# A fixed order for the expert pairs, with the gather one pair ahead and the overflow branch moved

## The chip, the cores and the metric

The kernel runs on one core of a Trainium2 chip (trn2). The metric is the device time of one execution in microseconds (us); less is better.

## The reference

One block of a network on 256 tokens of width 2048, all in float32. A vector `c` gives shifts, scales and gates through `silu(c) @ w_ada + b_ada`.

```
h  = rmsnorm(x) * (1 + sc1) + sh1;  proj = h @ w_in             # 2048 x 7192
mix = [gated delta rule (8 heads), forgetting attention (8 heads)] @ w_out
x  = x + g1 * mix
h2 = rmsnorm(x) * (1 + sc2) + sh2
# experts: top-1 of 4 groups, then top-2 of the 8 experts of that group
y  = sum over chosen e of weight_e * (silu(h2 @ w1[e]) * (h2 @ w3[e])) @ w2[e]
out = rmsnorm(x + g2 * y)
```

There are 32 experts, each with `w1` and `w3` of 2048 x 512 and `w2` of 512 x 2048: 12 MB an expert. Every expert's weights are read, whichever tokens chose it.

## The kernel before

**Start.** `mod_T(n)` makes four rows of the first shift and scale from weight tiles `mt` (1 MB each, `ada_load`, line 204): of each pair of tiles VectorE takes one (`ada_dve`, lines 215 and 217) and TensorE the other (line 229). Both need `sc_t`, which is silu(c): one ScalarE activation (line 172) and three small VectorE instructions. ScalarE issues loads ahead of that activation: the constants `KC`, four quarters `xq` of x, the further constants `K`, the parameters `SM`, three rows into `MOD`; later `wab` (line 480). After all of `mod_T(0)` come the 16 `x_transpose` (line 199) and `mod_fin(0)` (line 243), then the projection with weight tiles `wr` (line 361; ScalarE and VectorE split each into two parts, lines 371 and 377). In this part the order on TensorE and SyncE is the order in which the code is written (`manual_schedule`); elsewhere a list scheduler that works with estimated times lays out each engine's instructions at build time, and may take later ones ahead. A DMA can also wait for an earlier DMA whose completion semaphore it takes over.

**Experts.** 16 pairs of experts, each with 64 token slots per expert. One-hot matrices are built on VectorE: `oh` (line 1217), `ohr` (1223, with the norm's factor), `ohw` (1220, with the weights). The rest of a pair is, on TensorE:

- gather: four times 8 matmuls by `ohr` (line 1229) into the PSUM tag `g` (two buffers), added on VectorE into `heT` (line 1230). The first quarter comes ahead of the pair's up projection, the others between its quarters (`GA = 1`);
- up: 64 matmuls into `h1` and `h3` (line 1249), the two experts of the pair in the two column halves of the array, so that two matmuls run side by side;
- hidden: tanh on ScalarE (1255), two VectorE instructions (1256, 1257), four transposes `pht` (1260) and two `pwt` of `ohw` (1265), copied by ScalarE into `hidT` (1262) and `ow` (1267);
- down: 32 matmuls into `po` (1290; for the last pair 1309, column block by column block), scaled by the gate on VectorE (`scale_out`, 1279);
- scatter: 8 matmuls `py` (1273), added on VectorE into `X2` (1275).

The profile counts each float32 matmul as two records. SyncE loads the weights in tiles of 1 MB (lines 1244, 1286, 1306), 24 a pair, into a ring of 17 slots (`r2t` nine, `r3t` eight) and at the first turn three tiles that borrow other buffers (`r4t`).

Tokens beyond 64 of an expert are left to `overflow`, a branch on the greatest count (`tc.If`, line 1162) with a loop over all experts inside. It stands ahead of pair 8 (`OVP = 8`, pairs counted from 0), uses SyncE loads into `r2t`, and isn't entered with these inputs.

```
    for pr in range(NE // 2):
        e0 = 2 * pr
        if pr == OVP:
            overflow()
        ...
        for q in range(4):
            if q + GA < 4:
                gather(q + GA)
            for hx, wr in ((h1, w1_r), (h3, w3_r)):
                ...
```

Of the kernel before, what the change touches and what calls it, by code (L numbers as in the profile page):

```python
# [7 lines left out]
F32 = mybir.dt.float32  # L8
# [8 lines left out]
P = 128  # L17
# [52 lines left out]
OVP = 8  # L70
# [10 lines left out]
C_LATE, C_W = 320, 992 + 3 * 128  # L81
# [29 lines left out]
def block_kernel(ctx: ExitStack, tc: tile.TileContext, x, w_mod, w_gate, w_in, w_ab, w_out, w_router, w1, w3, w2,  # L111
# [45 lines left out]
    def kc(c0, n):  # L157
        return K[:, c0 - C_LATE:c0 - C_LATE + n]
# [7 lines left out]
    nc.scalar.dma_start(K, consts[:, C_LATE:])  # L166
    nc.scalar.dma_start(SM, small.partition_broadcast(P))
    nc.scalar.dma_start(MOD[0:P:32], rows[:, 0:3])
# [291 lines left out]
    for _ in mod_T(0):  # L460
        pass
    for j in range(NJ):
        x_transpose(j)
    mod_fin(0)
    n_rot = 0
    for b in range(3):
        b_now[0] = b
        m = mod_T(b + 1)
        for c in range(7):
            for _ in range(MP[c]):  # L470
                next(m)
            if c == 6:
                mod_fin(b + 1)
            if c == 0:
                step(acc_k, "T", hHb, hLb, 0, NJ - 1)
            else:
                spilled(early[c], c, b, rot[n_rot % 2])
                n_rot += 1
        if b == 1:
            nc.scalar.dma_start(wab[:, :, 0:24], w_ab)  # L480
# [662 lines left out]
    def ring2_tile():  # L1143
        n = ring_n[0]
        ring_n[0] += 1
        if RB + RC <= n < RB + RC + 3:
            tag, bufs = (("heT", 2), ("ob", 1), ("g2b", 1))[n - RB - RC]
            return ep.tile([P, 2048], F32, name="r4t", tag=tag, bufs=bufs)
        if n >= RB + RC:
            n -= 3  # L1150
        if n % (RB + RC) >= RB:
            return ring3.tile([P, 2048], F32, name="r3t", tag="r3t")
        return ring2.tile([P, 2048], F32, name="r2t", tag="r2t")
# [6 lines left out]
    def overflow():  # L1160
        most = nc.values_load(cnt[0:1, 0:1], min_val=0, max_val=T)
        with tc.If(most > CAP):  # L1162
            dr = ep.tile([P, 2, P], F32, name="dr", tag="ow", bufs=1)
            for t in range(2):
                nc.vector.tensor_scalar(dr[:, t], ident, r2[:, t:t + 1], None, op0=OP.mult)
            hv = [ep.tile([P, 8, T], F32, name="hv", tag="heT", bufs=2) for _ in range(2)]
            for j in range(0, NJ, 2):
                pt = ps_g.tile([P, 2, T], F32, name="pth", tag="g")
                for a in range(2):
                    for t in range(2):  # L1170
                        nc.tensor.matmul(pt[:, a, t * P:(t + 1) * P], h2p[:, t, j + a], dr[:, t], start=True, stop=True)
                nc.vector.tensor_tensor(hv[j // 8][:, j % 8:j % 8 + 2], pt,
                                        S2[:, j:j + 2, None].to_broadcast([P, 2, T]), op=OP.add)
            with tc.For_i(0, NE, 1) as e:
                hp = [[ps_o.tile([P, 512], F32, name="hx", tag="o") for t in range(2)] for m in range(2)]
                for m, wr in enumerate((w1_r, w3_r)):
                    for q in range(4):
                        tl = ring2.tile([P, 2048], F32, name="r2t", tag="r2t").rearrange("p (j f) -> p j f", j=4)
                        nc.sync.dma_start(tl, wr[bass.ds(e, 1), :, 4 * q:4 * q + 4].rearrange("o p j f -> p (o j) f"))
                        for jj in range(4):  # L1180
                            j = 4 * q + jj
                            for t in range(2):
                                nc.tensor.matmul(hp[m][t], hv[j // 8][:, j % 8, t * P:(t + 1) * P], tl[:, jj],
                                                 start=j == 0, stop=j == NJ - 1)
                hT = ep.tile([P, 4, T], F32, name="vhT", tag="ob", bufs=1)
                for t in range(2):
                    th = ep.tile([P, 512], F32, name="vth", tag="eth", bufs=1)
                    nc.scalar.activation(th, hp[0][t], AF.Tanh, scale=0.5)
                    nc.vector.scalar_tensor_tensor(th, th, 1.0, hp[0][t], op0=OP.add, op1=OP.mult)
                    nc.vector.scalar_tensor_tensor(th, th, 0.5, hp[1][t], op0=OP.mult, op1=OP.mult)  # L1190
                    nc.vector.tensor_scalar(th, th, cof[:, t, bass.ds(e, 1)], None, op0=OP.mult)
                    pt = ps_g.tile([P, 4, P], F32, name="vpt", tag="g")
                    for c in range(4):
                        nc.tensor.transpose(pt[:, c], th[:, c * P:(c + 1) * P], ident)
                    nc.scalar.activation(hT[:, :, t * P:(t + 1) * P], pt, AF.Copy)
                wt = []
                for c in range(4):
                    tl = ring2.tile([P, 2048], F32, name="r2t", tag="r2t").rearrange("p (o d) -> p o d", o=1)
                    nc.sync.dma_start(tl, w2_r[bass.ds(e, 1), :, c].rearrange("o p d -> p o d"))
                    wt.append(tl)  # L1200
                for n in range(4):
                    for t in range(2):
                        py = ps_g.tile([P, 512], F32, name="vpy", tag="g")
                        for c in range(4):
                            nc.tensor.matmul(py, hT[:, c, t * P:(t + 1) * P], wt[c][:, 0, n * 512:(n + 1) * 512],
                                             start=c == 0, stop=c == 3)
                        vy = ep.tile([P, 512], F32, name="vy", tag="eth", bufs=1)
                        nc.vector.tensor_tensor(vy, py, g2b[n], op=OP.mult)
                        xs = X2[:, t, n * 512:(n + 1) * 512]
                        nc.vector.tensor_tensor(xs, xs, vy, op=OP.add)  # L1210

    for pr in range(NE // 2):
        e0 = 2 * pr
        if pr == OVP:
            overflow()
# [3 lines left out]
        ohw = ep.tile([P, 2, 2, SLOTS], F32, name="ohw", tag="ohw", bufs=1)  # L1219
        nc.vector.tensor_tensor(ohw, oh, comb[:, :, e0:e0 + 2, None].to_broadcast([P, 2, 2, SLOTS]), op=OP.mult)  # L1220
        heT = ep.tile([P, NJ, P], F32, name="heT", tag="heT", bufs=2)
        ohr = ep.tile([P, 2, 2, SLOTS], F32, name="ohr", tag="ohr", bufs=2)
        nc.vector.tensor_tensor(ohr.rearrange("p t a s -> p t (a s)"), oh.rearrange("p t a s -> p t (a s)"),
                                r2[:, :, None].to_broadcast([P, 2, 2 * SLOTS]), op=OP.mult)
        def gather(j4):
            pg_ = ps_g.tile([P, 4, P], F32, name="pgt", tag="g")
            for jj in range(4):
                for t in range(2):
                    nc.tensor.matmul(pg_[:, jj], h2p[:, t, 4 * j4 + jj], ohr[:, t], start=t == 0, stop=t == 1)  # L1229
            nc.vector.tensor_tensor(heT[:, 4 * j4:4 * j4 + 4], pg_,  # L1230
                                    S2[:, 4 * j4:4 * j4 + 4, None].to_broadcast([P, 4, P]), op=OP.add)

        h1 = ps_h.tile([P, 512], F32, name="h1", tag="h")
        h3 = ps_h.tile([P, 512], F32, name="h3", tag="h")
        for j4 in range(GA):
            gather(j4)
        for q in range(4):
            if q + GA < 4:
                gather(q + GA)
# [11 lines left out]
        if pr == NE // 2 - 1:  # L1251
            fgt = ep.tile([P, 2048], F32, name="fgb", tag="heT", bufs=2)
            fgb = [bcast(fgt[:, n * 512:(n + 1) * 512], MOD[:, 1], n) for n in range(4)]
# [3 lines left out]
        nc.vector.scalar_tensor_tensor(th, th, 0.5, h3, op0=OP.mult, op1=OP.mult)  # L1257
        pt = ps_g.tile([P, 4, P], F32, name="pht", tag="g")
# [8 lines left out]
        nc.scalar.activation(ow, pw, AF.Copy)  # L1267
        po = [ps_o.tile([P, 512], F32, name="po", tag="o") for _ in range(4)]
# [12 lines left out]
        if pr < NE // 2 - 1:  # L1281
# [11 lines left out]
            if pr == 0:  # L1293
                g2t = ep.tile([P, 2048], F32, name="g2b", tag="g2b", bufs=1)
                g2b = [bcast(g2t[:, n * 512:(n + 1) * 512], MOD[:, 2], n) for n in range(4)]
            for n in range(4):
                scale_out(n)
            for t in range(2):
                for n in range(4):
                    scatter(t, n)  # L1300
        else:
            for n in range(4):
                wt = [ring2_tile().rearrange("p (c f) -> p c f", c=4) for _ in range(2)]
                for cs in (slice(0, 2), slice(2, 4)):
                    for i in range(2):
                        nc.sync.dma_start(wt[i][:, cs], w2_r[e0 + i, :, cs, n * 512:(n + 1) * 512])
                for c in range(4):
                    for i in range(2):
                        nc.tensor.matmul(po[n][64 * i:64 * i + 64], hT[:, c, 64 * i:64 * i + 64], wt[i][:, c],  # L1309
# [11 lines left out]
    for t in range(2):  # L1321
        for n in range(4):
# [7 lines left out]
            if n % 2:  # L1330
                nc.sync.dma_start(out[0, t * P:(t + 1) * P, (n - 1) * 512:(n + 1) * 512],
                                  X2[:, t, (n - 1) * 512:(n + 1) * 512])
    est.close()
# [51 lines left out]
```

## Time and profile before

| what | value |
|---|---|
| time, median of 3 runs | 1703.01 us (1700.43 to 1703.21) |
| the profiled execution: its own time | 1703.19 us |
| its span, first to last instruction | 1701.4 us |
| TensorE busy in the span | 1575.6 us (93%) |
| VectorE, ScalarE, GpSimd busy | 39%, 19%, 7% |
| DMA over the span | 588.50 MB, mean 346 GB/s |
| mean granted TensorE clock | 0.978 of full speed |

Busy shares are means over the span: TensorE waits in the first 50 us and in the last 40, and is all but always busy between. The span leaves 1.8 us of the execution's own time outside it.

### The profile page before, as it was taken

The page shows a single profiled execution, that of the slowest core. Times are in us where ns is not written, and L with a number is a line of the kernel's source. Part 1 is how long each engine was busy: PE and PEld are TensorE (multiplying, and loading weights), DVE is VectorE, ACT ScalarE, POOL GpSimd, SP SyncE. Part 2 cuts the span into 40 slices and gives each one's busy share as a digit, 9 for nine tenths or more (in the row PEclk, how much of TensorE's full clock was granted, in tenths as well). Part 3 has the DMA queues.
Part 4 walks back from the last instruction along what each step waited for, and adds up shares of the span by engine and source line. Part 5 has one row for each costly group of instructions (what it writes and reads, how often), then busy time and mean ns, then how long its engine had stood idle before and what let it go on. Part 6 is the DMA issues. An engine that isn't in the chain of part 4 may idle for free. (4 is left out here: it accounts for less than half of the span.)

```text
span 1701.4 us, 20695 instructions
## 1 busy us (share of the span) xinstructions
PE 1575.6 (93%) x8430; PEld 892.4 (52%) x8430; DVE 663.4 (39%) x1038; ACT 327.8 (19%) x652; POOL 116.5 (7%) x140
## 2 busy tenths in 40 slices
PE   3999988899899988799999999999899999999996
PEld 1788857787678766433433443443443443343342
DVE  4677797766655644220221221222022122122022
ACT  2543553353334543100000000000000000000002
POOL 1000041332101021000000000000000000000001
PEclk9999999899999999799999999999999999999999
DMA  9989787787786475799999999994999999999993
GB/s 348 367 331 352 266 315 287 266 316 274 290 314 244 148 294 207 311 385 387 407 406 421 405 407 421 405 406 163 385 420 421 420 421 420 421 421 420 421 408 115
DMA packets 102038, 588.50 MB, mean 346 GB/s; under 512 B 16932, under 2 KB 17316, under 8 KB 41268
## 3 DMA queue, kind: packets, MB, share of 16 engines
q1 hardware_dynamic: 93916, 581.05, 85.2%
q10 hardware_dynamic: 8024, 6.09, 1.2%
q8 instruction: 68, 1.11, 0.3%
q14 instruction: 30, 0.25, 0.0%
HBM read 584.73 MB, written 2.10 MB: 345 GB/s over the span
## 5 line engine op out<-in xcount | busy, mean ns | idle before, releaser
L1249 PE MATMUL h<-r2t,heT 128*64 128x512 f32 x1088 | 270.1, 595 | 1.9 <-DMA r2t<-in_w_dram 1.9
L1249 PE MATMUL h<-r3t,heT 128*64 128x512 f32 x960 | 240.0, 594 | 0.0
L377 DVE TENSOR_TENSOR wL<-wr,wH 128x1024 fp32r<-128x1024 f32 x144 | 176.9, 1231 | 96.7 <-ACT wH L371 81.3
L371 ACT ACTIVATE wH<-wr 128x1024 fp32r<-128x1024 f32 x144 | 151.6, 1056 | 144.3 <-PE acc L408 70.0
L1255 ACT ACTIVATE eth<-h 128x512 f32<-128x512 f32 x16 | 9.6, 597 | 880.0 <-PE h L1249 880.0
L1249 PEld LDWEIGHTS h<-r2t,heT 128*64 128x64 f32 x1088 | 84.1, 137 | 148.4 <-issue 141.0
L1230 DVE TENSOR_TENSOR heT<-pgt,S 128x512 f32<-128x512 f32 x64 | 44.3, 691 | 296.9 <-PE pgt L1229 296.9
L1229 PEld LDWEIGHTS pgt<-ohr,h2p 128*128 128x128 f32 x1024 | 120.6, 195 | 42.8 <-issue 32.3
L1249 PEld LDWEIGHTS h<-r3t,heT 128*64 128x64 f32 x960 | 75.2, 137 | 125.8 <-issue 122.8
L1229 PE MATMUL pgt<-ohr,h2p 128*128 128x128 f32 x1024 | 129.5, 283 | 6.2 <-PEq L1162 3.4
L1290 PE MATMUL po<-r2t,hidT 128*64 128x512 f32 x496 | 130.0, 597 | 4.2 <-ACT hidT L1262 4.2
L1273 PE MATMUL py<-ob,ow 128*128 128x512 f32 x256 | 123.4, 618 | 2.4 <-DVE ob L1279 2.3
L1290 PE MATMUL po<-r3t,hidT 128*64 128x512 f32 x440 | 121.1, 597 | 3.6 <-ACT hidT L1262 3.6
L1279 DVE TENSOR_TENSOR ob<-po,g2b 128x512 f32<-128x512 f32 x64 | 40.4, 684 | 213.1 <-PE po L1290 199.2
L404 PE MATMUL acc<-hH,wH 128*128 128x256 f32 x640 | 100.4, 297 | 12.0 <-ACT wH L371 12.0
L404 PE MATMUL acc<-hH,wL 128*128 128x256 f32 x640 | 97.2, 292 | 8.4 <-DVE wL L377 8.3
L1275 DVE TENSOR_TENSOR X<-X,py 128x512 f32<-128x512 f32 x128 | 88.0, 687 | 36.7 <-PE py L1273 36.7
L404 PEld LDWEIGHTS acc<-hH,wH 128*128 128x128 f32 x640 | 85.7, 197 | 27.2 <-ACT wH L371 16.9
L404 PE MATMUL acc<-hL,wH 128*128 128x256 f32 x640 | 97.0, 293 | 0.0
L404 PEld LDWEIGHTS acc<-hH,wL 128*128 128x128 f32 x640 | 85.4, 196 | 18.6 <-DVE wL L377 10.5
L404 PEld LDWEIGHTS acc<-hL,wH 128*128 128x128 f32 x640 | 86.2, 198 | 5.5 <-issue 5.0
L1290 PEld LDWEIGHTS po<-r2t,hidT 128*64 128x64 f32 x496 | 45.1, 137 | 77.4 <-issue 71.0
(348 smaller groups left out, 1496.7 us busy)
## 6 DMA issues: line engine op xcount, KB each, us to landing
r2t<-in_w_dram SPq DMA_DIRECT2D x198, 1024.0 KB
r3t<-in_w_dram SPq DMA_DIRECT2D x175, 1024.0 KB
at<-in_w_gate_dram SPq DMA_DIRECT2D x64, 1024.0 KB
wr<-in_w_in_dram SPq DMA_DIRECT2D x112, 512.0 KB
mt<-in_w_mod_dram SPq DMA_DIRECT2D x32, 1024.0 KB
wr<-in_w_out_dram SPq DMA_DIRECT2D x32, 512.0 KB
r2t<-in_w_dram SPq DMA_DIRECT2D x14, 512.0 KB
r4t<-in_w_dram SPq DMA_DIRECT2D x3, 1024.0 KB
```

The lines of the kernel that those rows point to most:

```text
L371: nc.scalar.activation(H, rw, AF.Copy)
L377: nc.vector.tensor_tensor(Lf[:, :cut], rf_[:, :cut], Hf[:, :cut], op=OP.subtract)
L404: nc.tensor.matmul(acc[b], wt[:, j - j0, b * P:(b + 1) * P], ht, start=st and b % 2 == 0, stop=sp_, skip_group_check=True)
L1229: nc.tensor.matmul(pg_[:, jj], h2p[:, t, 4 * j4 + jj], ohr[:, t], start=t == 0, stop=t == 1)
L1230: nc.vector.tensor_tensor(heT[:, 4 * j4:4 * j4 + 4], pg_, S2[:, 4 * j4:4 * j4 + 4, None].to_broadcast([P, 4, P]), op=OP.add)
L1249: nc.tensor.matmul(hx[64 * i:64 * i + 64], heT[:, j, 64 * i:64 * i + 64], wt[i][:, jj], start=j == 0, stop=j == NJ - 1, tile_position=(0, ...
L1255: nc.scalar.activation(th, h1, AF.Tanh, scale=0.5)
L1273: nc.tensor.matmul(py, ow[:, t], ob[:, n * 512:(n + 1) * 512], start=True, stop=True)
L1275: nc.vector.tensor_tensor(xs, xs, py, op=OP.add)
L1279: nc.vector.tensor_tensor(ob[:, n * 512:(n + 1) * 512], po[n], g2b[n], op=OP.mult)
L1290: nc.tensor.matmul(po[n][64 * i:64 * i + 64], hT[:, c, 64 * i:64 * i + 64], wt[i][:, n * 512:(n + 1) * 512], start=c == 0, stop=c == 3, ti ...
```

## The change

Start: the columns `C_STK` of the constants go from `K` to `KC`; the loads of `K`, `SM` and `MOD` become `late_loads`, issued by SyncE after `mod_fin(0)`, and `wab` is issued by SyncE too; eight `x_transpose` stand behind each of the second and third quarter of `mod_T(0)`.

Experts: the whole loop stands under `manual_schedule` for TensorE and SyncE, so that both run it as written. `routes`, `gather`, `up` and `turn` are functions; the gather of pair `pr + 1` stands between the up projection and the transposes of pair `pr` (the first pair gathers for itself as before). The last pair's down weights are loaded whole ahead of its transposes. One of the three borrowed buffers of the ring (`heT`) is given up.

Overflow: behind pair 2 (`OVP = 2`), one token half after the other, loads by GpSimd into the tag `ob`, no use of `r2t`; `preferred_fallthrough_block=False` asks that the code of the branch not taken follow directly.

```
-OVP = 8
+OVP = 2
...
-C_LATE, C_W = 320, 992 + 3 * 128
+C_LATE, C_W = 352, 992 + 3 * 128
...
-    nc.scalar.dma_start(K, consts[:, C_LATE:])
-    nc.scalar.dma_start(SM, small.partition_broadcast(P))
-    nc.scalar.dma_start(MOD[0:P:32], rows[:, 0:3])
+    def late_loads():
+        nc.sync.dma_start(K, consts[:, C_LATE:])
+        nc.sync.dma_start(SM, small.partition_broadcast(P))
+        nc.sync.dma_start(MOD[0:P:32], rows[:, 0:3])
...
-    for _ in mod_T(0):
-        pass
-    for j in range(NJ):
-        x_transpose(j)
+    m = mod_T(0)
+    for q in range(4):
+        next(m)
+        next(m)
+        if q in (1, 2):
+            for j in range(8 * q - 8, 8 * q):
+                x_transpose(j)
     mod_fin(0)
     n_rot = 0
+    late_loads()
...
-            nc.scalar.dma_start(wab[:, :, 0:24], w_ab)
+            nc.sync.dma_start(wab[:, :, 0:24], w_ab)
...
-        if RB + RC <= n < RB + RC + 3:
-            tag, bufs = (("heT", 2), ("ob", 1), ("g2b", 1))[n - RB - RC]
+        if RB + RC <= n < RB + RC + 2:
+            return ep.tile([P, 2048], F32, name="r4t", tag=("ob", "g2b")[n - RB - RC], bufs=1)
...
-        with tc.If(most > CAP):
+        with tc.If(most > CAP, preferred_fallthrough_block=False):
+            hv = ep.tile([P, NJ, P], F32, name="hv", tag="heT", bufs=2)
             for t in range(2):
+                overflow_half(t, hv)
+    def overflow_half(t, hv):
+        dr = ep.tile([P, P], F32, name="dr", tag="oh", bufs=1)
...
+                    tl = ep.tile([P, 4, 512], F32, name="vw", tag="ob", bufs=1)
+                    nc.gpsimd.dma_start(tl, wr[bass.ds(e, 1), :, 4 * q:4 * q + 4].rearrange("o p j f -> p (o j) f"))
...
-        ohw = ep.tile([P, 2, 2, SLOTS], F32, name="ohw", tag="ohw", bufs=1)
-        ohr = ep.tile([P, 2, 2, SLOTS], F32, name="ohr", tag="ohr", bufs=2)
+        ohr = ep.tile([P, 2, 2, SLOTS], F32, name="ohr", tag="ohr", bufs=1)
+        ohw = ep.tile([P, 2, 2, SLOTS], F32, name="ohw", tag="ohw", bufs=2)
...
+    order3 = ExitStack()
+    order3.enter_context(tc.manual_schedule(engines={ET.PE, ET.SP}))
+    g2b = []
+    route = routes(0)
+    heT = he_tile()
+    gather(route[0], heT, 0)
+    for pr in range(NE // 2):
+        e0 = 2 * pr
+        last = pr == NE // 2 - 1
+        th = up(pr, heT, None if pr else route[0])
+        if not last:
+            coming = routes(pr + 1)
+            heT = he_tile()
+            for j4 in range(4):
+                gather(coming[0], heT, j4)
+        else:
+            w2t = [ring2.tile([P, 2048], F32, name="r2t", tag="r2t").rearrange("p (c f) -> p c f", c=4)
+                   for _ in range(8)]
+            for n in range(4):
+                for cs in (slice(0, 2), slice(2, 4)):
+                    for i in range(2):
+                        nc.sync.dma_start(w2t[2 * n + i][:, cs], w2_r[e0 + i, :, cs, n * 512:(n + 1) * 512])
+        hT, ow = turn(th, route[1])
...
             for t in range(2):
                 for n in range(4):
                     scatter(t, n)
+            if pr == OVP:
+                overflow()
```

## Rows read from the trace of the kernel before

**Rows 1.** Windows: length, busy time of each engine, granted clock, DMA share, GB/s.

```profile
650.00:700.00 50.00, 35.44 (x158) 26.89 (x157) 21.76 (x62) 15.67 (x25) 6.28 (x6) 0.80 0.72 286
...
1195.00:1230.00 35.00, 33.08 (x175) 14.50 (x175) 3.45 (x5) 0.60 (x1) 0.00 (x0) 1.00 1.01 421
1230.00:1640.00 410.00, 400.62 (x1846) 168.80 (x1844) 91.83 (x143) 9.68 (x20) 2.92 (x4) 1.00 1.01 420
```

**Rows 2.** ScalarE's timeline, the tanh of pairs 7, 8 (start, us, instruction, [idle before]).

```profile
1160.82 0.60 ACT L1255 ACTIVATE eth<-h 128x512 f32<-128x512 f32 x1 [55.62 <-PE h L1249]
1228.59 0.60 ACT L1255 ACTIVATE eth<-h 128x512 f32<-128x512 f32 x1 [61.94 <-PE h L1249]
```

**Rows 3.** TensorE's timeline, one pair from its down projection to the next one's.

```profile
1417.26 0.66 PE L1260 MATMUL pht<-KC,eth 128*128 128x128 f32 x4 [0.82 <-DVE eth L1257]
...
1418.66 7.57 PE L1290 MATMUL po<-r2t,hidT 128*64 128x512 f32 x29 [0.53 <-ACT hidT L1262]
...
1434.54 7.70 PE L1273 MATMUL py<-ob,ow 128*128 128x512 f32 x16
1442.16 3.84 PE L1229 MATMUL pgt<-ohr,h2p 128*128 128x128 f32 x32
1445.93 7.09 PE L1249 MATMUL h<-r3t,heT 128*64 128x512 f32 x32
...
1454.93 7.09 PE L1249 MATMUL h<-r2t,heT 128*64 128x512 f32 x32
...
1463.93 7.51 PE L1249 MATMUL h<-r2t,heT 128*64 128x512 f32 x33
...
1478.70 0.66 PE L1260 MATMUL pht<-KC,eth 128*128 128x128 f32 x4 [0.82 <-DVE eth L1257]
```

**Rows 4.** TensorE's timeline in the first pair.

```profile
738.55 0.64 PE L1290 MATMUL po<-r3t,hidT 128*64 128x512 f32 x1 [0.47 <-ACT hidT L1262]
...
752.44 7.70 PE L1273 MATMUL py<-ob,ow 128*128 128x512 f32 x16
760.06 3.84 PE L1229 MATMUL pgt<-ohr,h2p 128*128 128x128 f32 x32
```

**Rows 5.** Weight loads of TensorE (PEld) in the down projection of rows 3.

```profile
1422.58 0.14 PEld L1290 LDWEIGHTS po<-r2t,hidT 128*64 128x64 f32 x1 [0.29 <-issue]
```

**Rows 6.** VectorE's timeline beside the down projection of rows 3.

```profile
1419.09 0.42 DVE L1223 TENSOR_TENSOR ohr<-oh,r 128x256 f32<-128x256 f32 x1
```

**Rows 7.** Instructions of line 1162, the branch (duration min/median/max ns).

```profile
L1162 PEldq COMPARE_BRANCH  x1: 3583/3583/3583, 1189.5 to 1189.5; - x1
L1162 DVEq COMPARE_BRANCH  x1: 72/72/72, 1190.7 to 1190.7; - x1
```

**Rows 8.** Waits of SyncE's queue, 1160 to 1215 us: total, times, longest.

```profile
SPq L1244 <- PEq L1162: 14.9, 1, 14.9
```

**Rows 9.** SyncE's timeline at the start of the stage of experts.

```profile
708.12 4.33 SPq L1286 DMA_DIRECT2D r2t<-in_w_dram  x4
```

**Rows 10.** TensorE's timeline, start of the kernel.

```profile
34.69 5.99 PE L199 MATMUL pt<-KC,xq 128*128 128x128 f32 x32
...
47.35 2.08 PE L404 MATMUL acc<-hH,wH 128*128 128x256 f32 x8 [3.80 <-ACT wH L371]
```

**Rows 11.** ScalarE's timeline, start of the kernel.

```profile
11.45 0.22 ACT L172 ACTIVATE sc_t<-V 128x16 f32<-128x16 f32 x1
```

**Rows 12.** Waits of SyncE's queue, first 60 us.

```profile
SPq L204 <- DMA xq<-in_x_dram: 14.2, 3, 8.6
SPq L361 <- DMA wab<-in_w_ab_dram: 9.9, 1, 9.9
```

**Rows 13.** DMA issues: queue, count, KB each.

```profile
K<-in_consts_dram ACTq DMA_DIRECT2D x1, 528.0 KB
wab<-in_w_ab_dram ACTq DMA_DIRECT2D x1, 192.0 KB
```

**Rows 14.** TensorE's timeline, last pair's down projection.

```profile
1664.40 0.64 PE L1309 MATMUL po<-r3t,hidT 128*64 128x512 f32 x1 [0.53 <-ACT hidT L1262]
```

## What the change was expected to do

> **What bounds the kernel now.** I read the windows first [rows 1]: in the expert stage TensorE is busy for 400.62 of 410 us while the DMA engines move 420 GB/s at a share of 1.01. Both look full, so the next question is which one the other waits for. A pair needs 24 tiles of 1.0486 MB; at 420 GB/s a tile takes 2.50 us and a pair 59.9 us. TensorE's timeline gives the pair's real period, from one `pht` to the next: 61.44 us [rows 3]. TensorE is therefore the bound there, and the loads, 1.5 us faster a pair, are made to wait by the ring.
>
> The period falls apart into pieces, from start to start [rows 3]: down 15.88, scatter 7.62, two quarters of the gather 3.77, a quarter of up with a quarter of the gather 9.00, the same again 9.00, the second half of up with the wait for the hidden values 14.77, the turn 1.40. They sum to 61.44. Two things in them are not work. The wait for the second VectorE instruction of the hidden values is 0.82. And the down projection took 13.89 us in the first pair [rows 4], against 15.88, with the same 32 matmuls. The two experts' matmuls are meant to run side by side, in the two column halves, so weights should be loaded in twos; in the later pair a single load (x1) stands at 1422.58 [rows 5]. The planner's order has let one half run ahead, and for some 1.99 us a half is alone.
>
> Pair 8 is the exception: its tanh comes 67.77 us after that of pair 7 [rows 2], 6.33 over the period. TensorE's branch takes 3583 ns, VectorE's 72 [rows 7], and SyncE waited 14.9 us for TensorE to have passed it [rows 8], so that the ring ran empty.
>
> At the start the chain is another. The transposes of x take 5.99 us on TensorE and stand behind the last matmul of the first modulation row; the first projection matmul comes at 47.35 [rows 10]. Ahead of that, silu(c) waits to 11.45 behind ScalarE's own loads [rows 11], and SyncE waits 9.9 us for `wab` to land [rows 12].
>
> **The pair, part by part.** The fixed order gives down 13.89 (pair 0 is the measure, same instructions, same tiles in a row): -1.99. With the whole gather of the next pair behind up, the 0.82 vanishes: 7 us of gather cover a chain of one VectorE instruction. Up in one piece is twice 13.95 (14.77 less 0.82), the gather in one piece twice 3.77; each doubled figure counts a change of operand that now occurs once, about 0.2 each, so I take 27.7 and 7.4. The turn stays 1.40: `pwt` may wait for the last quarter's addition, but the copy of `pht` that the down projection waits for is no later. Scatter stays 7.62. Sum: 27.7 + 7.4 + 1.40 + 13.89 + 7.62 = 58.0 us, against 61.44. Bounds of the 3.4: below, 1.99 alone with new waits for the two gather buffers eating the rest; above, 3.8 if the doubled pieces shrink more.
>
> Pair 1's gather began at 760.06 [rows 4]. In the new order that gather stands inside pair 0: up of pair 1 starts at 760.06 + 7.4 - 0.82 = 766.6. Fourteen periods of 58.0 bring up of pair 15 to 1578.6; 27.7, the 0.82 (the last pair has no gather to hide it) and 1.40 bring its down projection to 1608.5, against 1664.40 [rows 14]. From there the order of the last pair is the old one.
>
> **The branch.** Nothing of it runs on SyncE any more, and its buffers are not the ring's: the 14.9 us wait has no place. TensorE's 3.58 us go with the jump if the untaken code follows directly; the load of the count is issued while the last scatter matmuls still run. Price 0 to 3.6; I take 0, because VectorE's 72 ns [rows 7] is what a branch costs that finds its code. GpSimd, now in the branch, has no work before the last pair.
>
> **The loads now.** At 58.0 us a pair TensorE asks for more than 24 tiles in 59.9 us give. What covers the difference is the head start: 17 slots and three borrowed buffers are filled before the stage, and SyncE's next load, for the first slot that comes free, is at 708.12 [rows 9]. After the change it is 19 (one borrowed buffer less, 2.5 us), and 365 of 384 tiles remain: 365 x 2.497 = 911 us of moving. In the first pairs the ring is still full at times. Up of pair 0 with its own gathers frees 16 slots in 35 us and the loads fill 14, so the 9 us of gather and turn leave them some 4 us without a slot, and scatter another 1.5; from pair 1 on more is taken than comes. With 2 us from issue to the first data the last tile lands at 708.1 + 2 + 911 + 5.5 = 1626.6. Up of pair 15 ends with the ninth tile from the end: 1626.6 - 8 x 2.497 = 1606.6, 1.7 for its matmuls, 0.82 and 1.40 make the down projection start at 1610.5. That is 2 us behind TensorE's own 1608.5: the stage passes from one bound to the other, and I take the later. Gain 1664.4 - 1610.5 = 53.9 us.
>
> **The start.** Eight transposes each go into TensorE's waits for the second and third pair of tiles: 5.9 us leave the chain. `K` and `wab` are 528 and 192 KB [rows 13], 1.7 us at 420 GB/s, that no longer share the engines with the first tiles; they are issued by SyncE behind these, ahead of the next row's tiles, and delay them by as much. The 9.9 us wait for `wab` goes, but the first projection tile must then really be there some 6 us sooner, and the fill that was loaded during the old delay is thinner: I give 1.7 back. Net -6; bounds 0 (the first projection tiles late by all of it) and -8. What follows up to the experts is bound mostly by TensorE, and I let the gain through whole. The Trainium skill ("DMA: Bandwidth & Descriptors", "Queues, rings and completion order") says that SyncE and ScalarE each own one ring on every DMA engine and that a ring is consumed in order, which speaks against the move: small rows now stand ahead of weights. The trace agrees that small loads hold SyncE up [rows 12], though there from ScalarE's queue; by the rule alone the start would give 4 us and the time be 1645.
>
> **Sum.** The profiled execution took 1703.19 us (span 1701.4, 1.8 around it), 0.2 over the median of 1703.01. 1703.2 - 53.9 - 6 = 1643.
>
> **Rivals.**
> *SyncE loses its head start.* If it still waits at the branch for TensorE, or if the fixed order keeps it from loading before the stage, the ring is empty when up of pair 3 begins at 766.6 + 116 = 882.6, and 13 pairs of 24 tiles follow at 2.497: last landing 882.6 + 2 + 779 = 1663.6, 37 later: 1680. For it: today's 14.9 us wait [rows 8]. Against: that wait was for buffers of the ring.
> *The gather's operand is late.* If VectorE takes `oh` and `ohr` of the next pair in written order, behind the hidden values, TensorE waits 0.82 plus two instructions of 0.42, some 1.7 a pair; 14 pairs are 24 us, the stage ends 22 behind the forecast: 1665. Against: today `ohr` is made during the down projection, far ahead [rows 6].
> *The branch still jumps, or the start gives nothing.* 1643 to 1649; the loads hide 2 of the 3.6.
> *Slower than before: TensorE's clock falls.* Late pairs now wait for loads. At 650 to 700 us, after waits in the routing, the granted clock was 0.80 of full, 20 of 50 us at 1.2 GHz instead of 2.4, which costs 10 us of work [rows 1]. One such stretch in each of 14 pairs gives 1783; from six on the gain is gone. Against: from 1195 to 1230, with the ring empty and TensorE busy for 33.08 of 35 us, the clock stayed at 1.00 [rows 1]. The Trainium skill ("TensorE: Matmul & The Clock Gate", "HAM oscillation — how this bites in real kernels") describes a kernel whose waits for DMA bring the half clock back again and again; this window disagrees for waits of this size.
>
> **How the numbers follow.** Forecast with its bounds 0.78 (own range 1634 to 1650: down if up and gather join better, up if the start gives nothing); head start lost 0.09; late operand 0.07; clock 0.04; no change 0.02. The range reaches from 1633 to 1666, which takes in the late operand. A measurement here tells 0.2% from no change, 3.4 us. Faster 0.94, same 0.02, slower 0.04.
>
> **What would show it.** The first projection matmul near 41 us. A tanh every 58 us, later 60; down to scatter 13.9; `pht` without the 0.82 wait but in the last pair. No SyncE wait on line 1162 and a TensorE branch below 0.5 us. DMA at 420 GB/s without a break from about 770, with first waits of TensorE for tiles in the last third. Wrong would be: a period at 61, a hole in the DMA row behind pair 2, waits of the gather on VectorE, or a granted clock under 1.00 between 770 and 1600.

## The result and the profile after

The changed kernel takes 1657.98 us (median of 4 runs, 1656.68 to 1658.80) against 1703.11 of the kernel before beside it (4 runs, 1700.43 to 1704.61): ratio 0.9738, 95% interval 0.9726 to 0.975. The profiled execution took 1658.80, its span is 1657.1. That is faster, as forecast, and inside the range of 1633 to 1666, but 15 us above the 1643 of the sum and above the 1634 to 1650 that the main forecast gave itself. The profile shows which terms held and which did not.

ScalarE's timeline of the changed kernel gives the period of a pair by its tanh, as [rows 2] did (start, us, instruction, [idle before]); here pairs 1 to 4 and 12 to 15.

```profile
788.89 0.60 ACT L1257 ACTIVATE eth<-h 128x512 f32<-128x512 f32 x1 [45.36 <-PE h L1254]
846.63 0.60 ACT L1257 ACTIVATE eth<-h 128x512 f32<-128x512 f32 x1 [45.33 <-PE h L1254]
913.91 0.60 ACT L1257 ACTIVATE eth<-h 128x512 f32<-128x512 f32 x1 [54.87 <-PE h L1254]
971.67 0.60 ACT L1257 ACTIVATE eth<-h 128x512 f32<-128x512 f32 x1 [45.38 <-PE h L1254]
...
1433.52 0.60 ACT L1257 ACTIVATE eth<-h 128x512 f32<-128x512 f32 x1 [45.33 <-PE h L1254]
1492.28 0.60 ACT L1257 ACTIVATE eth<-h 128x512 f32<-128x512 f32 x1 [45.67 <-PE h L1254]
1551.90 0.60 ACT L1257 ACTIVATE eth<-h 128x512 f32<-128x512 f32 x1 [45.64 <-PE h L1254]
1613.11 0.60 ACT L1257 ACTIVATE eth<-h 128x512 f32<-128x512 f32 x1 [47.22 <-PE h L1254]
```

The period is 57.74 (846.63 - 788.89) where it was 61.44; of the pairs in the middle most take 57.73. Two things break it: pair 3, behind the branch, takes 67.28, which is 9.55 more than the 57.73 of the pairs after it; and the last three periods are 58.76, 59.62 and 61.21.

TensorE's timeline of the changed kernel, from the gather to the next up projection, answers to [rows 3].

```profile
849.92 7.41 PE L1231 MATMUL pgt<-ohr,h2p 128*128 128x128 f32 x64
857.17 0.60 PE L1265 MATMUL pht<-KC,eth 128*128 128x128 f32 x4
858.12 0.44 PE L1270 MATMUL pwt<-KC,ohw 128*128 128x128 f32 x2 [0.35 <-DVE heT L1232]
858.51 10.52 PE L1325 MATMUL po<-r3t,hidT 128*64 128x512 f32 x48
868.86 3.60 PE L1325 MATMUL po<-r2t,hidT 128*64 128x512 f32 x16
872.40 7.70 PE L1308 MATMUL py<-ob,ow 128*128 128x512 f32 x16
886.35 1.12 PE L1254 MATMUL h<-r2t,heT 128*64 128x512 f32 x2 [6.25 <-issue]
```

Gather to transposes is 7.25 (forecast 7.4), the turn 1.34 (1.40), down 13.89 (13.89), and `pht` has no wait in front of it. `pwt` waits 0.35 for VectorE's last addition, which costs nothing that was not in the sum. The last row is what the sum did not have: the up projection of pair 3 starts 6.25 us late, and the row names "issue", that is, no semaphore that it waited for.

The instructions of the branch's line in the changed kernel (duration min/median/max in ns), as [rows 7]:

```profile
L1170 PEldq COMPARE_BRANCH  x2: 95/3047/5999, 879.6 to 880.3; - x2
L1170 DVEq COMPARE_BRANCH  x2: 51/53/55, 880.8 to 881.0; - x2
```

There are two branch instructions now. TensorE's second one takes 5999 ns, more than the 3583 before. On VectorE, and by the same view on ScalarE, GpSimd and SyncE, they stay at 38 to 55 ns. SyncE does not wait at the branch any more.

Windows of the changed kernel, with the columns of [rows 1]:

```profile
730.00:770.00 40.00, 39.65 (x198) 18.00 (x196) 13.60 (x21) 1.58 (x3) 2.80 (x4) 1.00 0.89 348
770.00:872.00 102.00, 101.30 (x516) 43.36 (x512) 19.02 (x29) 3.15 (x6) 0.00 (x0) 1.00 1.01 421
872.00:905.00 33.00, 26.75 (x93) 9.68 (x91) 8.15 (x14) 0.00 (x0) 0.00 (x0) 0.90 0.88 361
...
885.20:892.10 6.90, 5.75 (x13) 1.53 (x15) 0.00 (x0) 0.00 (x0) 0.00 (x0) 0.51 0.65 270
...
905.00:1376.00 471.00, 468.21 (x2269) 195.24 (x2267) 108.70 (x168) 12.83 (x25) 0.00 (x0) 1.00 1.01 421
```

From 885.2 to 892.1 the granted clock is 0.51, the lower of the two levels. It falls while TensorE still stands; TensorE works in 5.75 of these 6.9 us, and half the clock takes about 2.9 us of work from them. With the 6.25 us of idleness that is 9.1 of the 9.55; the last 0.4 were not traced. The loads, at 421 GB/s before and after, fall to 361 in the 33 us from 872 to 905: 33 x (1 - 361/421) = 4.7 us of moving are lost for good. Both are among the prediction's own signs of being wrong: a hole in the DMA row behind pair 2, and a granted clock under 1.00 between 770 and 1600.

The start, by TensorE's timeline of the changed kernel, against [rows 10]:

```profile
42.02 2.07 PE L409 MATMUL acc<-hH,wH 128*128 128x256 f32 x8 [0.34 <-ACT wH L376]
...
52.15 1.75 PE L234 MATMUL ada<-mt,cbc 128*32 128x512 f32 x8 [2.60 <-DMA mt<-in_w_mod_dram]
```

The projection begins 5.33 us sooner (42.02 against 47.35), as forecast. silu(c) moved from 11.45 [rows 11] to 4.52. But 10 us later TensorE waits 2.60 for a weight tile. Its granted clock from 45 to 60 is 0.87; it was 0.77 there in the kernel before, so the clock is not what takes the gain away. The 76th record of the projection, which stood at 59.55 before, is only 1.54 sooner. SyncE's waits of the first 62 us, against [rows 12]:

```profile
SPq L209 <- DMA mt<-in_w_mod_dram: 14.1, 3, 7.6
SPq L366 <- DVE wL L382: 12.8, 6, 5.8
...
SPq L366 <- DMA SM<-in_small_dram: 1.6, 1, 1.6
...
SPq L366 <- DMA K<-in_consts_dram: 0.7, 1, 0.7
```

The 9.9 for `wab` is gone. In its place stand waits for buffers of the projection tiles, and two for the small loads that now go ahead of the projection tiles.

The end, by TensorE's timeline of the last pair, against [rows 14]:

```profile
1614.43 3.65 PE L1254 MATMUL h<-r3t,heT 128*64 128x512 f32 x14 [1.36 <-DMA r3t<-in_w_dram]
1618.86 0.65 PE L1265 MATMUL pht<-KC,eth 128*128 128x128 f32 x4 [0.78 <-DVE eth L1259]
...
1620.26 3.65 PE L1342 MATMUL po<-r2t,hidT 128*64 128x512 f32 x16 [0.53 <-ACT hidT L1267]
```

The down projection of the last pair starts at 1620.26, where the sum of the prediction had 1610.5 less 6 for the start, 1604.5. All of the miss lies ahead of this row: from here to the end of the span it is 36.8 us, before it was 37.0 (1701.4 - 1664.40).

### The profile page after: what moved, and what is told of

Same layout as the page of the kernel before. It is cut to its first block, busy times and chain, and to the rows that moved or that the text cites. A ratio compares the mean times of both kernels' runs of the same rounds, so it can differ in the third digit from the quotient of the medians.

```text
span 1657.1 us, 20657 instructions
## 1 busy us (share of the span) xinstructions
PE 1542.3 (93%) x8430; PEld 877.5 (53%) x8430; DVE 665.7 (40%) x1038; ACT 329.9 (20%) x652; POOL 117.2 (7%) x140
## 5 line engine op out<-in xcount | busy, mean ns | idle before, releaser
L1254 PE MATMUL h<-r2t,heT 128*64 128x512 f32 x1088 | 265.9, 599 | 7.1 <-issue 6.2
L1254 PE MATMUL h<-r3t,heT 128*64 128x512 f32 x960 | 235.6, 593 | 3.1 <-DMA r3t<-in_w_dram 3.1
L1258 DVE SCALAR_TENSOR_TENSOR eth<-eth,h 128x512 f32<-128x512 f32 x16 | 11.0, 687 | 381.7 <-ACT eth L1257 381.7
L1231 PE MATMUL pgt<-ohr,h2p 128*128 128x128 f32 x1024 | 121.0, 279 | 2.5 <-DVE ohr L1221 2.5
L1325 PE MATMUL po<-r2t,hidT 128*64 128x512 f32 x496 | 122.9, 593 | 0.0
L1314 DVE TENSOR_TENSOR ob<-po,g2b 128x512 f32<-128x512 f32 x64 | 44.2, 691 | 182.6 <-PE po L1325 166.7
L1325 PE MATMUL po<-r3t,hidT 128*64 128x512 f32 x448 | 112.6, 594 | 0.0
L1308 PEld LDWEIGHTS py<-ob,ow 128*128 128x128 f32 x256 | 39.7, 188 | 87.0 <-DVE X L1310 59.0
```

The costliest lines, as they stand in the source:

```text
L1254: nc.tensor.matmul(hx[64 * i:64 * i + 64], heT[:, j, 64 * i:64 * i + 64], wt[i][:, jj], start=j == 0, stop=j == NJ - 1, tile_position=(0, ...
L1258: nc.vector.scalar_tensor_tensor(th, th, 1.0, h1, op0=OP.add, op1=OP.mult)
L1308: nc.tensor.matmul(py, ow[:, t], ob[:, n * 512:(n + 1) * 512], start=True, stop=True)
L1314: nc.vector.tensor_tensor(ob[:, n * 512:(n + 1) * 512], po[n], g2b[n], op=OP.mult)
```

## The experiments

Three questions were open: what the branch costs and why, where the start's 5.3 us went, and whether the last periods are long because of the loads. All diffs are against the changed kernel unless the text says otherwise; `...` stands for lines left out. Ratios are to the kernel before on the same chip. A row with one run has no interval, and four runs of one kernel lay up to 6 us apart (1655.32 to 1661.38 for the changed kernel, once more), so of those rows the traces are read and not the times.

| kernel | time us, runs | ratio, 95% interval |
|---|---|---|
| changed | 1657.98, 4 | 0.9738, 0.9726 to 0.975 |
| no branch | 1653.83, 4 | 0.9706, 0.9675 to 0.9736 |
| branch behind pair 12 | 1656.78, 4 | 0.973, 0.9704 to 0.9756 |
| no fall-through flag | 1657.5, 1 | |
| half a body | 1651.47, 1 | |
| branch behind pair 7 | 1653.84, 5 | 0.9713, 0.9693 to 0.9733 |
| old start | 1661.04, 4 | 0.9758, 0.9736 to 0.978 |
| before, with the new start | 1702.44, 10 | 1.0006, 0.9992 to 1.002 |
| fixed order alone | 1671.43, 4 | 0.9829, 0.9805 to 0.9853 |
| late small loads | 1654.6, 1 | |
| 23 tiles a pair | 1636.89, 1 | |
| branch behind pair 7, late small loads | 1649.70, 5 | 0.9689, 0.9672 to 0.9705 |
| changed, once more | 1659.36, 4 | 0.9744, 0.972 to 0.9767 |

### No branch

```
-            if pr == OVP:
-                overflow()
```

> The changed kernel without the overflow branch (the tokens beyond 64 of an expert are left out; with these inputs there are none). In the changed kernel's profile pair 3 takes 67.28 us against 57.73 of its neighbours: TensorE stands still for 6.25 us at the branch, and in 885.2 to 892.1 us its clock is granted at half. Theory: that is the whole of the 9.55 us, and all of it goes, but the kernel ends with the loads as the bound (the last three periods are 58.8, 59.6 and 61.2 us), and the loads only lost the 4.7 us for which they stood still beside the branch (361 GB/s for 33 us against 421). So 1653 to 1654, with more of the last pairs at 59.8 us. Rival, TensorE bound to the end: 1648.5. Rival, the branch hidden already: 1658.

Measured: 1653.83. ScalarE's timeline of this kernel, pairs 2, 3, 10, 11 and 15:

```profile
846.34 0.60 ACT L1257 ACTIVATE eth<-h 128x512 f32<-128x512 f32 x1 [45.33 <-PE h L1254]
904.08 0.60 ACT L1257 ACTIVATE eth<-h 128x512 f32<-128x512 f32 x1 [45.33 <-PE h L1254]
...
1308.20 0.60 ACT L1257 ACTIVATE eth<-h 128x512 f32<-128x512 f32 x1 [45.33 <-PE h L1254]
1367.22 0.60 ACT L1257 ACTIVATE eth<-h 128x512 f32<-128x512 f32 x1 [45.63 <-PE h L1254]
...
1607.27 0.60 ACT L1257 ACTIVATE eth<-h 128x512 f32<-128x512 f32 x1 [45.66 <-PE h L1254]
```

Pair 3 takes 57.74, so all 9.55 us are the branch's. Long periods begin with pair 11 (59.02) and not with pair 13, so some of the time is given back: the last tanh is 5.84 us sooner. The branch costs 9.55 where it stands and 5.8 at the last tanh. The medians are 4.2 apart, and the intervals of the two ratios overlap a little, so the cost at the end rests on the traces.

### The branch behind pair 12

```
-OVP = 2
+OVP = 12
```

> The changed kernel with the branch behind pair 12 in place of pair 2. Theory: the branch costs TensorE the same 9 to 10 us there, but by then the ring has been drawn down by one tile a pair or so, the loads go on while TensorE stands, and no time of the loads is lost: 1653 to 1654, as without the branch. Rival, the branch costs its 9.5 us wherever it stands: 1658. Rival, the stall comes on top, since the loads are just in time there: 1662.

Measured: 1656.78, a miss. ScalarE's timeline of this kernel, pairs 12, 13 and 15:

```profile
1428.64 0.60 ACT L1257 ACTIVATE eth<-h 128x512 f32<-128x512 f32 x1 [46.77 <-PE h L1254]
1496.02 0.60 ACT L1257 ACTIVATE eth<-h 128x512 f32<-128x512 f32 x1 [53.39 <-PE h L1254]
...
1611.45 0.60 ACT L1257 ACTIVATE eth<-h 128x512 f32<-128x512 f32 x1 [45.30 <-PE h L1254]
```

Pair 13 takes 67.38, and the two pairs left after it run at 57.73 and 57.70, no longer at the pace of the loads. So the stall is made up only in part: the last tanh comes at 1611.45, 1.7 sooner than in the changed kernel and 4.2 later than without a branch. The loads kept moving through it (419 GB/s from 1440 to 1475).

### No fall-through flag

```
-        with tc.If(most > CAP, preferred_fallthrough_block=False):
+        with tc.If(most > CAP):
```

> The changed kernel without preferred_fallthrough_block=False, so that the branch is laid out as in the kernel before (there TensorE had one taken branch of 3.58 us; in the changed kernel it has a first one of 0.1 us and a second of 6.0 us). Theory: with or without the flag TensorE has to jump over the body once and its code must be fetched: one branch instruction of 3.5 to 6 us, and with it 57.73 + 3 to 9.5 us from the tanh of pair 2 to that of pair 3. Rival, the flag makes the stall: no TensorE branch over 0.5 us. Rival, the flag already saves something: over 9.6 us on pair 3.

Measured: 1657.5. The branch's line of this kernel:

```profile
L1170 PEldq COMPARE_BRANCH  x1: 6047/6047/6047, 878.4 to 878.4; - x1
```

One instruction instead of two, and as long: 6047 against 5999. The flag changes the number of branches and not the price on TensorE.

### Half a body

The body of the branch, which isn't entered, holds one token half instead of two:

```
-            for t in range(2):
-                overflow_half(t, hv)
+            overflow_half(0, hv)
```

> The changed kernel with one token half in the branch's body instead of two (the second half's tokens beyond 64 of an expert are left out; there are none with these inputs). Theory, the stall is the fetch of code behind a jump: it depends on where the jump lands, not on the work jumped over, so it is either still 3 to 6 us or, if the target is now within what is fetched already, below 0.5 us; nothing between. Rival, the stall grows with the body: 3.0 us, half of 6.0.

Measured: 1651.47. The branch's line of this kernel:

```profile
L1170 PEldq COMPARE_BRANCH  x2: 95/200/304, 877.7 to 878.4; - x2
```

304 ns in place of 5999, pair 3 takes 58.35, and the clock is not halved. The price is not in proportion to what the branch passes over: half the body costs a twentieth. The Trainium skill ("Runtime: NRT & Kernel Launch", "Instruction fetch mechanics") says that a jump to code that isn't already at hand has to wait until that code is fetched. That fits these two rows, and the view of the DMA queues (queue, kind: packets, MB, share of 16 engines) shows what came in meanwhile. From the start of TensorE's second branch to its end in the changed kernel (880.3 to 886.3; two of the three rows), in the same stretch of the kernel before (1189.5 to 1193.1), and across both branches of half a body (877.7 to 878.8):

```profile
q1 hardware_dynamic: 336, 2.46, 99.4%
q8 instruction: 1, 0.02, 1.1%
...
q8 instruction: 1, 0.02, 1.5%
...
q1 hardware_dynamic: 63, 0.48, 103.5%
```

With a whole body instructions come in while TensorE stands at the branch, with half a body none. Narrower windows put the start of the packet on q8 at 883.8 in the changed kernel, 3.5 us after the branch began, and at 1190.7 in the kernel before, 1.2 us after. These 2.3 us are nearly all of the 2.4 between 5999 and 3583. The number of matmuls is not the reason for that difference: written out, the two bodies hold the same 136. What differs beside the packet is the loads, which stood still in the kernel before (5 GB/s, the packet alone) and moved 414 GB/s in the changed one. That the loads hold the packet up is likely but not shown, since no run stops them at the changed kernel's branch; nor does the view say whose instructions the packet carries.

### The branch behind pair 7

```
-OVP = 2
+OVP = 7
```

> The changed kernel with the branch behind pair 7. Behind pair 2 the ring was full and the loads stood still during the stall; behind pair 12 (1656.8 us) three pairs were too few to make up 9.7 us at 2 us a pair. Theory: behind pair 7 the ring has room for the stall and seven pairs or more follow, so that TensorE is back at the loads' pace before the end: the tanh of pair 15 within 1 us of 1607.3, where the kernel without the branch has it, and 1653 to 1654. Rival, the stall costs 4 us wherever it stands: 1657 to 1658.

Measured: 1653.84. As expected. The branch takes 5964 ns and pair 8 65.72, but the last tanh stands at 1608.22, 0.95 behind that of the kernel without a branch. A window of this kernel around the stall shows why:

```profile
1160.00:1200.00 40.00, 33.79 (x132) 10.77 (x130) 8.18 (x14) 0.00 (x0) 0.00 (x0) 0.91 1.01 420
```

TensorE loses its 6 us and the clock, but the loads go on at 420 GB/s: by then the ring has free slots. After pair 2 it was full (SyncE waited 26.6 of the 33 us for the up projection to free slots), and the loads fell to 361. A stall of TensorE in the middle is paid out of the time that TensorE would have waited for tiles later; early it takes loads along, late nothing is left to pay it with.

### The old start

The start of the kernel before (loads by ScalarE, transposes behind the modulation row), everything else changed:

```
-    def late_loads():
-        nc.sync.dma_start(K, consts[:, C_LATE:])
...
+    nc.scalar.dma_start(K, consts[:, C_LATE:])
...
-            nc.sync.dma_start(wab[:, :, 0:24], w_ab)
+            nc.scalar.dma_start(wab[:, :, 0:24], w_ab)
```

> The changed kernel with the start of the kernel before (loads of K, SM, MOD and wab by ScalarE, all transposes of x behind the first row). Theory: the start's gain of 5.3 us at the first projection matmul is given back by 60 us, since the stream of loads is the bound there, and 0.6 to 1.8 us of it reach the experts: 1659 to 1660. Rival, the start is worth its 5 us in the end: 1663.

Measured: 1661.04, 1 us above the theory's 1660 and 2 below the rival's 1663; the interval overlaps with that of the changed kernel, so the time does not decide. The first tanh comes at 730.95, against 731.25, and SyncE's first load of the experts' stage at 705.98, against 706.27: the experts begin no later with the old start. The 2 us by which both kernels begin them sooner than the kernel before (733.09 and 708.12) are thus not the start's, as far as one trace of each can tell.

### The kernel before with the new start

> The kernel before with only the start changed. Theory: first projection matmul near 42 us instead of 47.35, the difference shrinking to some 1.5 us by 60 us, and 1701 to 1702.5 in the end. Rival, the start is worth 5 us: 1698.

The edit is the part of the change ahead of the experts, in the kernel before. Measured: 1702.44, ratio 1.0006. The first projection matmul is at 42.51, the 76th record 0.15 sooner than before, the first tanh at 733.12 against 733.09. By itself the start gives nothing that these runs can tell from noise (at most 1.4 us by the interval).

### Late small loads

```
-    late_loads()
...
+        if b == 0:
+            late_loads()
```

The loads of `K`, `SM` and `MOD` stand behind the first round of the projection, no longer ahead of it.

> The changed kernel with the loads of K, SM and MOD moved from ahead of the first round of the projections to behind it. Theory: the stream of weight loads is the bound of the first 60 us, and the 0.65 MB of these three (about 1.6 us of the stream at 421 GB/s) take it from the weights that TensorE waits for at 52; without them the matmul that stood at 59.55 before comes 3 to 4.5 us earlier than there and not 1.5. Whether that reaches the experts is open: the first tanh by the theory at 730 to 731 (changed kernel 731.25), the time 1655 to 1658. Rival, the small loads cost nothing: the matmul still 1.5 us earlier, time 1658.

Measured: 1654.6. TensorE's timeline of this kernel:

```profile
49.16 1.06 PE L234 MATMUL ada<-mt,cbc 128*32 128x512 f32 x8 [0.36 <-DMA mt<-in_w_mod_dram]
```

The wait of 2.60 is 0.36, and the 76th record is 6.1 sooner than before, more than the theory asked for. SyncE no longer waits for a small load in this stretch. The edit takes away both the small loads' bytes and these waits, and does not tell which counted. In the nine kernels with the changed start as it is, the same record stands 0.0 later to 3.3 sooner. At the first tanh the gain is less clear: 727.05 here, 726.5 to 731.4 in those nine. In between lies the stage of attention and routing, whose waits differ from run to run (the changed kernel itself came to 731.25 and, once more, to 729.97).

### The fixed order alone

The order written out as in the change, but each pair gathers for itself, between its own quarters of up, as before:

```
...
-        th = up(pr, heT, None if pr else route[0])
-        if not last:
-            coming = routes(pr + 1)
-            heT = he_tile()
-            for j4 in range(4):
-                gather(coming[0], heT, j4)
-        else:
+        route = routes(pr)
+        heT = he_tile()
+        gather(route[0], heT, 0)
+        th = up(pr, heT, route[0])
+        if last:
...
```

> The changed kernel with the gather where it was (first quarter ahead of up, the others between its quarters), so that of the pair's edits only the fixed order remains. Theory: down takes 13.9 us as in the first pair before, the wait of 0.8 us for the hidden values and the joins remain: a period of 59.4 to 59.5 us against 61.44 before and 57.73 in the changed kernel, and 1674 to 1679, since the loads no longer bind at the end. Rival, the order does nothing by itself: 61.4 us a pair and 1700.

Measured: 1671.43. ScalarE's timeline of this kernel:

```profile
1151.61 0.60 ACT L1257 ACTIVATE eth<-h 128x512 f32<-128x512 f32 x1 [53.64 <-PE h L1254]
1211.05 0.60 ACT L1257 ACTIVATE eth<-h 128x512 f32<-128x512 f32 x1 [53.64 <-PE h L1254]
```

The period is 59.44, in the expectation's 59.4 to 59.5, and the down projection takes 13.89. The order is worth 2.00 of 61.44, the gather one pair ahead 1.71 more. The time is 2.6 us below the 1674 to 1679 that was expected; this kernel's first tanh stood at 726.53, 4.7 sooner than in the changed kernel, which accounts for it.

### 23 tiles a pair

```
                for i in range(2):
+                    if q == 3 and wr is w3_r and i == 1:
+                        wt.append(wt[0])
+                        continue
```

and no branch. The result is no longer that of the reference: a quarter of one matrix is replaced by the other expert's.

> No branch, and one of the 24 weight tiles of a pair isn't loaded (the last quarter of the second expert's third matrix takes the first expert's tile, which changes that part of the computation). Theory: the last pairs of the kernel without the branch have periods of 59 to 61 us because their tiles arrive late; with 23 tiles a pair the loads need 57.4 us a pair, less than TensorE's 57.73, so all periods are 57.7 and the last tanh comes at about 1597 instead of 1607, the time 1644 to 1646. Rival, the long periods of the last pairs are TensorE's own or those of the gather: periods still 59 to 61, time 1652 to 1654.

Measured: 1636.89. ScalarE's timeline of this kernel, pairs 14 and 15:

```profile
1535.05 0.60 ACT L1260 ACTIVATE eth<-h 128x512 f32<-128x512 f32 x1 [45.32 <-PE h L1257]
1592.75 0.60 ACT L1260 ACTIVATE eth<-h 128x512 f32<-128x512 f32 x1 [45.30 <-PE h L1257]
```

Every period is 57.6 to 57.7, to the last. The rival, that the long periods belong to TensorE or the gather, falls: with 24 tiles the last pairs wait for loads. Of the 16.5 us between the spans of this kernel and of the one without a branch (1635.1 and 1651.6), 10.5 are periods, 4.0 an earlier first tanh (726.96 against 730.97), and 2.0 the last pair. The expectation of 1644 to 1646 had the first of these alone, so as a time it is a miss.

### Branch behind pair 7, late small loads, and the changed kernel beside it

The two edits above together, and the changed kernel as it is.

> The branch behind pair 7 and the three small loads behind the first round of the projections. Theory: the branch is hidden behind the loads as it was with the branch behind pair 7 alone (1653.8), and the start gives up to 2 us more if the loads bind there: 1651 to 1654. Rival, the start's gain does not reach the experts: 1654.

> The changed kernel once more on the chip of these runs, to compare with: 1656 to 1659 by every theory; the kernel with the branch behind pair 7 and late small loads 3 to 6 us below it.

Measured: 1649.70 and 1659.36 on one chip, the first 1.3 below what was expected, the second 0.4 above, and 9.7 apart where 3 to 6 stood; the intervals of their ratios, 0.9672 to 0.9705 and 0.972 to 0.9767, are apart. ScalarE's timeline of the first of the two, pairs 0, 7, 8 and 15:

```profile
725.14 0.60 ACT L1258 ACTIVATE eth<-h 128x512 f32<-128x512 f32 x1 [39.86 <-PE h L1255]
...
1129.17 0.60 ACT L1258 ACTIVATE eth<-h 128x512 f32<-128x512 f32 x1 [45.33 <-PE h L1255]
1195.02 0.60 ACT L1258 ACTIVATE eth<-h 128x512 f32<-128x512 f32 x1 [53.45 <-PE h L1255]
...
1602.69 0.60 ACT L1258 ACTIVATE eth<-h 128x512 f32<-128x512 f32 x1 [46.68 <-PE h L1255]
```

The first tanh is 7.95 sooner than before, most of the 65.85 of pair 8 is made up for, and the last tanh is 9.1 sooner than in the changed kernel beside it (1611.76). Of these, 4.8 are there at the first tanh already (729.97 beside it), which differs that much between runs of the same start. This is the fastest of the versions that leave nothing out. Against the branch behind pair 7 alone it gains 4 us; the intervals of those two overlap a little, and the runs are from two chips.

## Why the forecast was right, and 15 us off

**Where luck came in.** The forecast's own range, 1634 to 1650, missed the time. The wide one, up to 1666, holds it only because it was drawn to take in a late gather operand, and that did not occur.

**The pair held.** 58.0 was forecast, 57.73 came. The order gave 2.00 (1.99 forecast); gather, turn and up came out at 7.25, 1.34 and 27.63, the last as what 57.73 leaves beside the others, where 7.4, 1.40 and 27.7 stood. The wait of 0.82 went, and the rival of a late gather operand did not occur: its two VectorE instructions were early enough, and the 0.35 at `pwt` lies inside the turn.

**The branch failed.** "Price 0 to 3.6; I take 0" was the wrong end and too short a range: TensorE's branch takes 6.0 us, the clock at half some 2.9 more, and 5.8 of the 9.55 are left at the last tanh. The value was taken from VectorE's 72 ns, while TensorE's own row in the same group [rows 7] showed 3583. The step "TensorE's 3.58 us go with the jump if the untaken code follows directly" did not hold: with the flag or without it TensorE waits 6 us. The rival "the branch still jumps, or the start gives nothing" is what happened, in both halves, but 1649 was too low for it: it priced the branch at the 3.6 of a kernel whose loads stood still. That SyncE's 14.9 us wait had no place any more was right.

**The start failed in the step "I let the gain through whole".** The projection did begin 5.3 us sooner, but the stage behind it took tiles faster than they came (417 GB/s from 45 to 60, and the wait of 2.60). The prediction gave 1.7 back for the small loads and called what follows bound mostly by TensorE; in the changed kernel all but 1.5 of the gain was gone at 60 us, and with the small loads out of the way 6.1 were left. Nor is TensorE all but always busy behind it: from 200 to 700 us of the kernel before it worked 446 of 500 us, so there are waits enough in which a gain can be lost. At the experts no share of the start is seen: they begin as soon with the old one. The rule of the Trainium skill that the prediction weighed ("DMA: Bandwidth & Descriptors", "Queues, rings and completion order": a ring is taken in order) was the better guide here: the prediction read from it that small loads hold up the weights behind them. Even the 4 us that it made of it were too many.

**The loads' part was right in kind, and too small.** The stage does pass from TensorE to the loads in its last third, the DMA engines run at 421 GB/s, and one tile less makes the long periods go. Step by step, for the kernel without a branch, whose last down projection starts at 1614.38 against 1604.5: the first load of the stage, forecast 6 sooner than 708.12 [rows 9], was at 706.00, which is 3.9 late; the last tile of up landed 4.0 later than this first load and the rate had it, 1.5 of that because the ring stood full for 7.0 us between 740 and 770 and not for 5.5 (396, 347 and 224 GB/s in three windows of 10 us); the last 2.5 were not traced. From its landing, at which TensorE goes on, to the down projection it took 5.8 and not 3.9, since 14 matmul records followed it:

```profile
1608.55 3.65 PE L1254 MATMUL h<-r3t,heT 128*64 128x512 f32 x14 [0.83 <-DMA r3t<-in_w_dram]
```

The branch adds 5.9: 9.9 + 5.9 = 15.8, the whole miss at 1620.26.

**The other rivals.** SyncE kept its head start: the ring was full between 740 and 770. A fall of TensorE's clock did take place, but once, behind the branch, for 6.9 us; the waits for tiles at the end (0.9 and 1.4 us) left it at 1.00. So the case on the slower side had a real mechanism, and the stalls that it needs did not come in each pair.

## What to carry to other kernels

Price a branch by the row of the engine that paid most at it, here TensorE, and not by the cheapest; take into account whether loads run at that place (3.3 to 3.6 us without, 5.9 to 6.2 with them), and add the half clock behind the longer stall. Put it where the tile ring has free slots and enough work is left that will wait for loads. When two limits are within a few per cent of each other (57.73 us of TensorE and 24 x 1.0486 MB at 421 GB/s, 59.8 us, of loads a pair), a stall of one costs at the end what the slack beside the other does not take up: 5.8 behind pair 2, 0.95 behind pair 7, 4.2 behind pair 12. A load of half a megabyte moved off one critical wait can land on the next one, so look up what stands behind it in the ring's order.

## What was not expected of the hardware

A branch around code that isn't entered cost TensorE 5999 ns with the whole body, 304 ns with half of it, and the other engines 38 to 55 ns. In all kernels with the whole changed body it was 5939 to 6240, with loads at 412 GB/s or more; with the body of the kernel before and the loads at a standstill it was 3583, and 3307 in the kernel before with the new start. Packets of instructions came in during each of the long ones, and none during the short one. The 6.25 us of idleness that it made were followed by 6.9 us at the half clock, in the middle of a stage that had run at 1.00; the 3583 ns of the kernel before were followed by 1.00 [rows 1].
